# A two-layer decoder trunk on one core: weight loads queued 3 steps further ahead, turned blocks read 5 steps on, a rebuilt layer change, and matmul operands at one place modulo 512 bytes

## The chip, the cores and the metric

The kernel runs on one core of one Trainium2 chip. The metric is the device time of one execution in microseconds, as the median over several runs. A profile of one execution (the page, and the trace behind it) shows what each engine did in it: TensorE (PE, with its weight loads as PEld), VectorE (DVE), ScalarE (ACT), and SyncE (SP), whose queue issues nearly all DMAs here.

## What is computed

256 tokens of width 2048 pass through two layers. Every layer has one input projection (2048 to 4096 columns: branch input, branch gate, memory query, memory gate), a memory attention of 4 heads into 256 memory tokens, a branch mixer (layer 0: trailing-window pooling; layer 1: causal attention of 12 heads, which at 256 tokens is one block), an output projection and a post-norm. Cut to what matters:

```python
h = x
for i in range(2):
    if i == 1:
        k, v = split(h @ w_kv_shared)                  # shared keys and values
    u = h @ w_in[i]
    branch_in, gate_b, mem_q, gate_m = split(u)
    branch = multiscale_pool(branch_in, pool_w, pool_scale) if i == 0 \
        else causal_attention(branch_in, k, v)
    mem_o = memory_attention(mem_q, mem, w_mem_kv[i])  # 4 heads, softmax over 256
    mixed = concat(branch * silu(gate_b), mem_o * silu(gate_m))
    y = mixed @ w_out[i]
    h = layer_norm(1.414 * h + y, ln_g[i], ln_b[i])
```

All of it is float32. Each product is made of three matmuls on operands that are split in two halves: high by high, high by low, low by high.

## The kernel before

**Items.** The weights are read in blocks of 128 partitions by 1024 floats (512 KB). One block is one item, a step of the program's main loop (`run`, L124). An item passes four stations: its load on SP's queue into one of 4 `raw` buffers; a split on ACT (`wh`, L63) and DVE (`wl`, L64) into one of 4 buffer pairs; 12 matmuls of 512 columns on PE (L59); and, after the eighth item of a projection, a consumer of the two finished accumulators. Three tables of numbers set the order: in step `i` the program writes down the split of item `i + LP` (3 ahead), then the load of item `i + LD` (4 ahead), then the matmuls of item `i`, then whatever earlier steps have put off to this one with `later`. Each engine, and SP's queue, runs its part in that order. A split of item `i + 3` needs a free `wh`/`wl` pair, that is, the end of the matmuls of item `i - 1`.

**Turned blocks.** A projection leaves rows of tokens; the next product needs columns. `turned` (L200) transposes 32 by 32 blocks on DVE into a tile `tr` (L184), and `spread` (L186) sends `tr` through DRAM: 4 DMAs out to `via` (L193) one step later, one DMA back (L196) two steps later, into the tile `dd`. Three steps after the transposes the block is read (`put`): split for queries and keys (`to_heads`), or put through tanh for gates (`to_gate`). Softmax weights make the same trip from and into the tile `p`.

**Attention.** `plan` (L380) puts off the stages of a pair of heads from the end of the query projection: scores `a`, exponentials, division, transposes `b`, split `halves` and the product with the values `c`. For memory pairs these are steps 4, 5, 6, 7, 10, 13 and 10, 11, 12, 13, 16, 18.

**Layer change.** After the last output projection of layer 0, `between` (L641) goes through four chunks of 512 columns: it loads gain and bias of the chunk (`ln_load`, on SP's queue), normalises it for both token halves on DVE (`norm_chunk`, two passes each, L422 and L423), transposes it, sends it through DRAM and splits it into `xT`. PE meanwhile works on the 16 items of the memory keys and values of layer 1, which do not need `xT`.

**Output projections.** `out_0` and `out_1` go through one group of 512 columns after the other, 8 items each.

**Place of the tiles.** The tiles lie one behind the other in each partition, each rounded up to 32 bytes. `gap` (384 bytes) puts the activations `xT`, `memT`, `zT` (16384 bytes for each half) at a multiple of 512 bytes. Behind them stand `res`, `ident` and `mask` (multiples of 512 together), `psc` (64), `eps_t` (32), `stats` (256) and `inv` (256): 608 bytes, so `raw`, `wh` and `wl`, and `tr`, `vv`, `kk`, `qq` behind them, begin 96 bytes past a multiple of 512. `ph` and `pl`, behind four more small tiles, begin 224 bytes past one. In the last stretch (`last`, L725) the weights of the final 512 output columns lie in the place of `xT` and `memT`, at a multiple of 512 bytes, and the stationary operand is `zT`, as in the rest of the output projection.

Of the kernel before, what the change touches and what calls it, by code (L numbers as in the profile page):

```python
# [17 lines left out]
P = 128  # L18
# [17 lines left out]
LD = 4  # L36
# [6 lines left out]
def trunk(ctx: ExitStack, tc: tile.TileContext, a: dict, out: bass.AP):  # L43
# [7 lines left out]
    sb.tile([P, 96], F32, name="gap")  # L51
# [134 lines left out]
    def spread(tr, n, first, land):  # L186

        st = {}

        def out():  # L190
            st["via"] = dr.tile([4, 32, 4, n], F32, name="via", bufs=3)
            for i in range(4):
                nc.sync.dma_start(st["via"][:, :, i].rearrange("j r x -> r j x"), tr[32 * i:32 * i + 32, :, :n])  # L193
# [6 lines left out]
    def turned(put, first=1):  # L200
# [20 lines left out]
    def to_heads(dst, first=1):  # L221
        def put(d):
            q = dst()
            split(in_order(q[:, 0]), in_order(q[:, 1]), d)
        return turned(put, first)
# [20 lines left out]
    class Rows:  # L246


        def maxima(self, parts):
            self.nb = sb.tile([P, 4], F32, name="nb", bufs=2)  # L250
            self.sm = sb.tile([P, 4], F32, name="sm", bufs=2)
# [23 lines left out]
    class MemPair(Rows):  # L275
# [19 lines left out]
        def b(self):  # L295
# [7 lines left out]
            spread(tr, 256, 1, lambda: self.d)  # L303
# [20 lines left out]
    class MobaPair(Rows):  # L324
# [24 lines left out]
        def b(self):  # L349
# [6 lines left out]
            spread(tr, 192, 1, lambda: self.d)  # L356
# [44 lines left out]
    def norm_stats(t, n):  # L401
        mv = sb.tile([P, 2], F32, name="mv", bufs=2)
        nc.vector.bn_aggr(mv, stats[:, t, :n].rearrange("p a b -> p (a b)"))
        rs = sb.tile([P, 1], F32, name="rs", bufs=2)
# [23 lines left out]
    psc = sb.tile([P, 12], F32, name="psc")  # L428
    eps_t = sb.tile([P, 4], F32, name="eps_t")
# [7 lines left out]
    def constants():  # L437
        nc.scalar.dma_start(ident, a["ident"])
# [30 lines left out]
    def mem_k(layer, first=1):  # L469
        k = fresh("k", lambda: heads_tile("kk"))  # L470
        proj(memT, halves(a["w_mk"][layer], 0), to_heads(k, first))
# [24 lines left out]
    def mem_q_gate(layer):  # L496
# [5 lines left out]
        def go():  # L502
            plan(prs[0], 4, 7, 10, 13)
            plan(prs[1], 10, 13, 16, 18)
# [94 lines left out]
    def out_0(n):  # L599
        proj(zT, [a["w_out"][0, n, kb] for kb in range(8)], to_residual(n), KORDER)  # L600
# [9 lines left out]
    weave(collect(out_0, 0), mixes[2] + mixes[3], 5)  # L610
    for n in range(1, 4):
        out_0(n)


    gbs = {}

    def ln_load(n):
        gbs[n] = load_gb(n)

    def ln0(n, t):  # L620
        norm_chunk(n, t, gbs[n])

    def h_turn(n):
# [5 lines left out]
        d = {}  # L629

        def land():
            d["d"] = sb.tile([P, 4, 256], F32, name="dd")
            return d["d"]

        def put():
            hi, lo = (in_order(x[:, 4 * n:4 * n + 4]) for x in xT)
            split(hi, lo, d["d"].rearrange("p i (e c) -> p e i c", c=32))
        spread(tr, 256, 1, land)
        later(3, put)

    def between():  # L641
        for n in range(4):
# [6 lines left out]
    mem_k(1, 7)  # L649
# [4 lines left out]
    for grp in range(3):  # L654
# [8 lines left out]
        def go(prs=prs):  # L663
            plan(prs[0], 4, 7, 10, 17)
            plan(prs[1], 10, 14, 18, 20)
# [3 lines left out]


    def out_1():
        for n in range(3):
            proj(zT, [a["w_out"][1, n, kb] for kb in range(8)], to_residual(n), KORDER)

# [4 lines left out]
    def load_gb_rows():  # L679
# [3 lines left out]
        gbt["sel"] = sb.tile([5, 2], F32, name="sel")  # L683
# [13 lines left out]
    for j, it in enumerate(collect(out_1)):  # L697
        items.append(it)
        if j == 0:
# [51 lines left out]
    m0 = sb.tile([P, 2], F32, name="m0")  # L751

# [23 lines left out]
    mv = sb.tile([P, 2], F32, name="mv", bufs=2)  # L776
    nc.vector.bn_aggr(mv, stats[:, 1].rearrange("p a b -> p (a b)"))
    rs = sb.tile([P, 1], F32, name="rs", bufs=2)
# [78 lines left out]
```

## Time and profile before

| | |
|---|---|
| median of 3 runs | 875.21 us (874.09 to 877.88) |
| the profiled execution's own time | 874.49 us |
| its span, first to last instruction | 872.7 us |
| mean granted TensorE clock | 0.979 |
| PE busy | 827.5 us (95% of the span) |
| DVE busy, ACT busy | 550.9 us (63%), 383.4 us (44%) |
| moved by DMA | 193.68 MB, mean 222 GB/s |

The busy time of PE overlaps from matmul to matmul, so how fast it goes is read from the starts of the matmuls, and how long it waits from the view of waits. The view of waits names for each wait the operation that ended it. The chain is the row of operations that ended last, followed back from the end. The granted clock (PEclk) is the share of full speed at which TensorE was allowed to run in a stretch. In the order of a program, rows are instructions of one engine in the order in which they stand, and `x4` is four equal ones; times are never read from it.

### The profile page before, as it was taken

How to read it: one execution, taken by the hardware profiler on the slowest of the kernel's cores; microseconds unless marked ns; L12 is line 12 of the kernel's file. 1: busy time of each engine (PE TensorE's matmuls, PEld its weight loads, DVE VectorE, ACT ScalarE, POOL GpSimd, SP SyncE). 2: the span in 40 equal slices, each digit the busy share in tenths (PEclk: the TensorE clock that was granted, in tenths of full speed). 3: DMA queues.
4: the chain of work that ended last, by engine and by line, in shares of the span. 5: the costliest groups of instructions: out<-in, count | busy, mean ns of one | idle time of the engine just before them, and what ended most of it. 6: DMA issues, size and time to landing. Idle time of an engine off the chain costs nothing.

```text
span 872.7 us, 10083 instructions
## 1 busy us (share of the span) xinstructions
PE 827.5 (95%) x3670; PEld 668.5 (77%) x3670; DVE 550.9 (63%) x705; ACT 383.4 (44%) x476; POOL 0.2 (0%) x4
## 2 busy tenths in 40 slices
PE   7999998999999999987899899999999998999996
PEld 6868786887788788865678678888788887888885
DVE  6655665668765655766565565675467654678746
ACT  6543443444544433423544454444345443445520
POOL 0000000000000000000000000000000000000000
PEclk9999999999999999999999989999999998999998
DMA  8877568766788665587875686777767676776842
GB/s 311 274 223 226 181 200 274 231 204 207 225 269 286 223 190 187 157 260 223 274 239 172 199 258 223 224 230 227 222 192 232 207 234 209 223 238 194 294 138 97
DMA packets 96117, 193.68 MB, mean 222 GB/s; under 512 B 8639, under 2 KB 31423, under 8 KB 95807
## 3 DMA queue, kind: packets, MB, share of 16 engines
q1 hardware_dynamic: 94800, 190.61, 69.0%
q10 hardware_dynamic: 1268, 2.44, 0.9%
q8 instruction: 28, 0.46, 0.2%
q14 instruction: 21, 0.17, 0.1%
HBM read 173.36 MB, written 19.66 MB: 221 GB/s over the span
## 4 chain that ended last, share of the span: by engine, by line
PE 61%; DMA 19%; DVE 10%; ACT 4%; SPq 3%; issue 3%; DVEq 0%; ACTq 0%
PE acc L59 58%; DMA via<-tr 6%; DMA raw<-in_w_in 5%; DVE wl L64 4%; DMA dd<-via 3%; SPq L193 3%; ACT wh L63 3%; DVE tr L184 2%; PE o L59 2%; PE s L59 2%; DMA raw<-in_w_mv 1%; DMA p<-via 1%; DMA raw<-in_w_mk 1%; DMA raw<-in_w_out 1%; DMA raw<-in_w_sk 1%
## 5 line engine op out<-in xcount | busy, mean ns | idle before, releaser
L64 DVE TENSOR_TENSOR wl<-raw,wh 128x1024 fp32r<-128x1024 f32 (+2 forms) x272 | 323.8, 1197 | 239.5 <-ACT wh L63 237.1
L63 ACT ACTIVATE wh<-raw 128x1024 fp32r<-128x1024 f32 (+2 forms) x272 | 280.9, 1038 | 340.7 <-PE acc L59 144.3
L59 PE MATMUL acc<-wl,xh 128*128 128x512 f32 x704 | 281.6, 400 | 5.1 <-DVE wl L64 5.1
L59 PE MATMUL acc<-wh,xh 128*128 128x512 f32 x704 | 281.8, 400 | 3.4 <-ACT wh L63 3.4
L59 PE MATMUL acc<-wh,xl 128*128 128x512 f32 x704 | 281.2, 400 | 0.0
L59 PEld LDWEIGHTS acc<-wl,xh 128*128 128x128 f32 x704 | 134.3, 191 | 39.8 <-DVE wl L64 8.0
L59 PEld LDWEIGHTS acc<-wh,xh 128*128 128x128 f32 x704 | 134.4, 191 | 36.2 <-ACT wh L63 4.7
L59 PEld LDWEIGHTS acc<-wh,xl 128*128 128x128 f32 x704 | 134.1, 190 | 32.3
L59 PE MATMUL acc<-wh,zl 128*128 128x512 f32 x224 | 88.7, 396 | 0.5 <-DVE zl L64 0.5
L59 PE MATMUL acc<-wl,zh 128*128 128x512 f32 x224 | 88.8, 396 | 0.0
L59 PE MATMUL acc<-wh,zh 128*128 128x512 f32 x224 | 88.2, 394 | 0.0
L59 PE MATMUL acc<-wh,mh 128*128 128x512 f32 (+1 forms) x130 | 53.3, 410 | 8.2 <-ACT wh L63 8.2
L59 PE MATMUL acc<-wl,mh 128*128 128x512 f32 (+1 forms) x130 | 53.2, 409 | 4.8 <-DVE wl L64 4.8
L59 PE MATMUL acc<-wh,ml 128*128 128x512 f32 (+1 forms) x130 | 52.4, 403 | 0.0
L59 PEld LDWEIGHTS acc<-wh,zl 128*128 128x128 f32 x224 | 42.1, 188 | 10.8 <-DVE zl L64 0.9
L59 PEld LDWEIGHTS acc<-wl,zh 128*128 128x128 f32 x224 | 42.1, 188 | 10.2
L59 PEld LDWEIGHTS acc<-wh,zh 128*128 128x128 f32 x224 | 42.1, 188 | 10.2
L59 PEld LDWEIGHTS acc<-wh,mh 128*128 128x128 f32 x130 | 25.8, 198 | 15.6 <-ACT wh L63 9.9
L59 PEld LDWEIGHTS acc<-wl,mh 128*128 128x128 f32 x130 | 25.6, 197 | 12.2 <-DVE wl L64 6.6
L59 PEld LDWEIGHTS acc<-wh,ml 128*128 128x128 f32 x130 | 25.7, 198 | 5.8
L184 DVE STREAM_TRANSPOSE tr<-acc 128x512 f32<-128x512 f32 x42 | 27.6, 693 | 1.3 <-PE acc L59 1.3
L63 ACT ACTIVATE zh<-zf 128x256 fp32r<-128x256 f32 x32 | 13.0, 415 | 31.4 <-DVE zf L272 26.7
(130 smaller groups left out, 532.7 us busy)
## 6 DMA issues: line engine op xcount, KB each, us to landing
raw<-in_w_in SPq DMA_DIRECT2D x128, 512.0 KB, 5.9
raw<-in_w_out SPq DMA_DIRECT2D x64, 512.0 KB, 4.4
via<-tr SPq DMA_DIRECT2D x116, 128.0 KB, 2.6
dd<-via SPq DMA_DIRECT2D x25, 512.0 KB, 4.4
raw<-in_w_sk SPq DMA_DIRECT2D x24, 512.0 KB, 5.6
raw<-in_w_sv SPq DMA_DIRECT2D x24, 512.0 KB, 5.1
raw<-in_w_mk SPq DMA_DIRECT2D x14, 512.0 KB, 5.6
raw<-in_w_mv SPq DMA_DIRECT2D x13, 512.0 KB, 5.8
```

The costliest lines, as they stand in the source:

```text
L59: nc.tensor.matmul(o, l, r, start=start, stop=stop)
L63: nc.scalar.activation(hi, src, AF.Copy)
L64: nc.vector.tensor_sub(lo, src, f(hi))
L184: nc.vector.transpose(dst, src)
L193: nc.sync.dma_start(st["via"][:, :, i].rearrange("j r x -> r j x"), tr[32 * i:32 * i + 32, :, :n])
```

## The change

1. `LD` goes from 4 to 7: in step `i` the load of item `i + 7` is written down, with the 4 `raw` buffers as they were.
2. `spread` writes the 4 DMAs out at once, in the step of the transposes, and the DMA back one step later. `turned` reads the block 5 steps after the transposes.
3. `plan` takes two numbers: scores at `a`, transposes at `a + 3`, `halves` at `a + 8`, the product with the values at `c`. Memory pairs: 6 and 16, 15 and 25; layer 1's pairs: 6 and 17, 15 and 25.
4. The layer change no longer normalises with gain and bias ahead of the turn. ACT normalises the chunk in place (`normed`, two instructions of 128 by 512 per chunk); it is transposed and sent through DRAM into the `gate` or `p` tile; ACT applies gain and bias there by column (`affine`, four instructions of 128 by 256 per chunk, from the new tile `gcol`), and the split follows a step later. The rows of `res` get gain and bias on DVE (`ln_rows`, four instructions per chunk) from step 20 on, and the loads for that stand at step 18 on. `gcol` is filled near the program's start by two DMAs on ACT's queue that read single floats.
5. The first two column groups of an output projection are interleaved (`out_cols`): 6 items of the one, 6 of the other, then the last two of each, which read the parts of `zT` that are finished last. The load of the final norm's rows moves from the first item to the eleventh.
6. `gap`, and the small tiles `nb`, `sm`, `mv`, `rs`, `m0` and `sel`, go; `psc` (64 bytes), `eps_t` (32), `gcol` (128) and one tile `small` (160) that holds the others stand ahead of `xT`: 384 bytes, as much as `gap` had. What is left between `mask` and `raw` is `stats` and `inv`, 512 bytes, so `raw`, `wh`, `wl`, `tr`, `vv`, `kk`, `qq`, `p`, `gate`, `ph` and `pl` all begin at a multiple of 512.

```diff
-LD = 4
+LD = 7
...
-    sb.tile([P, 96], F32, name="gap")
+    psc = sb.tile([P, 12], F32, name="psc")
+    eps_t = sb.tile([P, 4], F32, name="eps_t")
+    gcol = sb.tile([P, 2, KT], F32, name="gcol")
+    small = sb.tile([P, 40], F32, name="small")
...
-    def spread(tr, n, first, land):
+    def spread(tr, n, land):
...
-        later(first, out)
-        later(first + 1, back)
+        out()
+        later(1, back)
...
-                spread(st["tr"], 256, first, land)
-                later(first + 2, lambda: put(st["d"].rearrange("p i (e c) -> p e i c", c=32)))
+                spread(st["tr"], 256, land)
+                later(5, lambda: put(st["d"].rearrange("p i (e c) -> p e i c", c=32)))
...
-    def plan(pr, a, b, h, c):
+    def plan(pr, a, c):
...
-        later(b, pr.b)
-        later(h, pr.halves)
+        later(a + 3, pr.b)
+        later(a + 8, pr.halves)
         later(c, pr.c)
...
-            plan(prs[0], 4, 7, 10, 13)
-            plan(prs[1], 10, 13, 16, 18)
+            plan(prs[0], 6, 16)
+            plan(prs[1], 15, 25)
...
+        for i, nm in enumerate(("ln_g", "ln_b")):
+            nc.scalar.dma_start(gcol[:, i], a[nm][0].rearrange("(k p) -> p k", p=P))
...
+    def out_cols(layer, *ns, extra=()):
+        cols = [collect(proj, zT, [a["w_out"][layer, n, kb] for kb in range(8)], to_residual(n), KORDER)
+                for n in ns]
+        for c in cols:
+            items.extend(c[:6])
+        items.extend(extra)
+        for c in cols:
+            items.extend(c[6:])
...
-    weave(collect(out_0, 0), mixes[2] + mixes[3], 5)
-    for n in range(1, 4):
-        out_0(n)
+    main = collect(out_cols, 0, 0, 1)
+    items.extend(main[:5] + mixes[2] + mixes[3] + main[6:11] + main[5:6] + main[11:])
+    for n in range(2, 4):
+        out_cols(0, n)
...
+    def normed(n):
+        for t in range(2):
+            r = res[:, t, n * 512:(n + 1) * 512]
+            nc.scalar.activation(r, r, AF.Identity, scale=mvs[:, t, 2:3], bias=mvs[:, t, 3:4])
...
+        def affine():
+            for m in range(4):
+                y = d[:, :, m * 64:(m + 1) * 64]
+                nc.scalar.activation(y, y, AF.Identity, scale=gcol[:, 0, 4 * n + m:4 * n + m + 1],
+                                     bias=gcol[:, 1, 4 * n + m:4 * n + m + 1])
...
-        spread(tr, 256, 1, land)
-        later(3, put)
+        spread(tr, 256, lambda: d)
+        later(5, affine)
+        later(6, put)
...
-            later(3 * n, lambda n=n: ln_load(n))
-            later(1 + 3 * n, lambda n=n: ln0(n, 0))
-            later(2 + 3 * n, lambda n=n: ln0(n, 1))
+            later(1 + 3 * n, lambda n=n: normed(n))
             later(2 + 3 * n, lambda n=n: h_turn(n))
+            later(18 + 4 * n, lambda n=n: gbs.setdefault(n, load_gb(n)))
+            later(20 + 4 * n, lambda n=n: ln_rows(n, gbs[n]))
```

The order of SP's queue at the layer change, where the memory keys of layer 1 (`w_mk`) give way to the memory values (`w_mv`). Before, `ln_g` and `ln_b` are the gain and bias of a chunk, `via<-tr` the 4 DMAs out of a turned chunk, `dd<-via` its DMA back:

```order
L92 DMA raw<-in_w_mk 128x2x512 x4
L414 DMA ln_g<-in_ln_g 128x512
L414 DMA ln_b<-in_ln_b 128x512
L92 DMA raw<-in_w_mk 128x2x512 x3
L414 DMA ln_g<-in_ln_g 128x512
L414 DMA ln_b<-in_ln_b 128x512
L193 DMA via<-tr 32x4x256 x4
L92 DMA raw<-in_w_mk 128x2x512
L196 DMA dd<-via 128x1024
L94 DMA raw<-in_w_mv 128x1024 x2
```

The same place now; the chunk's DMA back lands in `gate` or `p`:

```order
L99 DMA raw<-in_w_mk 128x2x512 x8
L101 DMA raw<-in_w_mv 128x1024
L200 DMA via<-tr 32x4x256 x4
L101 DMA raw<-in_w_mv 128x1024
L203 DMA gate<-via 128x1024
L101 DMA raw<-in_w_mv 128x1024 x2
L200 DMA via<-tr 32x4x256 x4
L101 DMA raw<-in_w_mv 128x1024
L203 DMA p<-via 128x1024
```

The first chunk's DMAs out stood behind 7 loads of `w_mk` and two pairs of gain and bias; they now stand behind all 8 and the first of `w_mv`, and the gain and bias have left the place.

ACT's order at the same place. Before, `rs` is the root of the variance, `wh<-raw` the split of an item, `xh<-dd` that of a turned chunk:

```order
L405 ACT_TABLE_LOAD
L405 ACTIVATE rs<-mv,eps_t 128x1 x2
L63 ACTIVATE wh<-raw 128x1024 x5
L63 ACTIVATE xh<-dd 128x1024
L63 ACTIVATE wh<-raw 128x1024 x3
L63 ACTIVATE xh<-dd 128x1024
```

Now; `res<-res,small` is `normed`, `gate<-gate,gcol` and `p<-p,gcol` are `affine`:

```order
L410 ACTIVATE small<-small,eps_t 128x1 x2
L70 ACTIVATE wh<-raw 128x1024
L637 ACTIVATE res<-res,small 128x512 x2
L70 ACTIVATE wh<-raw 128x1024 x3
L637 ACTIVATE res<-res,small 128x512 x2
L70 ACTIVATE wh<-raw 128x1024 x3
L637 ACTIVATE res<-res,small 128x512 x2
L651 ACTIVATE gate<-gate,gcol 128x4x64 x4
L70 ACTIVATE wh<-raw 128x1024
L70 ACTIVATE xh<-gate 128x1024
L70 ACTIVATE wh<-raw 128x1024 x2
```

The first turned chunk is split behind 8 item splits instead of 5, and 6 instructions of `normed` and 4 of `affine` stand ahead of it.

More of the change, by code (lines that the diff above doesn't have):

```diff
@@ L196, in back, with turned @@
             nc.sync.dma_start(land(), st["via"].rearrange("j r i x -> (j r) i x"))
-        later(first, out)
-        later(first + 1, back)
-    def turned(put, first=1):
+        out()
+        later(1, back)
+    def turned(put):
         st = {}
@@ L219, in in_order, with to_heads @@
         return tile.rearrange("p a (t i c) -> p (a t) i c", t=2, i=4)
-    def to_heads(dst, first=1):
+    def to_heads(dst):
         def put(d):
@@ L224, in put @@
             split(in_order(q[:, 0]), in_order(q[:, 1]), d)
-        return turned(put, first)
+        return turned(put)
     def to_gate(dst):
@@ L302, in b @@
             self.d = self.p.rearrange("p j n -> p (j n)").rearrange("p (i x) -> p i x", i=4)
-            spread(tr, 256, 1, lambda: self.d)
+            spread(tr, 256, lambda: self.d)
         def halves(self):
@@ L467, in val_tile, with mem_k @@
         return sb.tile([P, 2, 2, 512], F32R, name="vv")
-    def mem_k(layer, first=1):
+    def mem_k(layer):
         k = fresh("k", lambda: heads_tile("kk"))
-        proj(memT, halves(a["w_mk"][layer], 0), to_heads(k, first))
+        proj(memT, halves(a["w_mk"][layer], 0), to_heads(k))
     def mem_v(layer):
@@ L609, in trunk, with ln_rows @@
     after(load_x)
-    weave(collect(out_0, 0), mixes[2] + mixes[3], 5)
-    for n in range(1, 4):
-        out_0(n)
[L615 to L621, printed above, removed]
+    main = collect(out_cols, 0, 0, 1)
+    items.extend(main[:5] + mixes[2] + mixes[3] + main[6:11] + main[5:6] + main[11:])
+    for n in range(2, 4):
+        out_cols(0, n)
+    def ln_rows(n, gb):
+        for t in range(2):
+            r = res[:, t, n * 512:(n + 1) * 512]
+            later(t, lambda r=r: nc.vector.tensor_tensor(r, r, gb[0], op=ALU.mult))
+            later(t, lambda r=r: nc.vector.tensor_add(r, r, gb[1]))
+    def normed(n):
+        for t in range(2):
+            r = res[:, t, n * 512:(n + 1) * 512]
+            nc.scalar.activation(r, r, AF.Identity, scale=mvs[:, t, 2:3], bias=mvs[:, t, 3:4])
     def h_turn(n):
@@ L628, in h_turn @@
                    res[:, t, n * 512:(n + 1) * 512].rearrange("p (m j c) -> p m j c", m=4, j=4))
[L629 to L633, printed above, removed]
+        d = sb.tile([P, 2, 512], F32, name="p") if n % 2 else gate_tile()
+        d = d.rearrange("p a b -> p (a b)").rearrange("p (i x) -> p i x", i=4)
+        def affine():
[3 more added lines that the diff above has]
+                                     bias=gcol[:, 1, 4 * n + m:4 * n + m + 1])
         def put():
             hi, lo = (in_order(x[:, 4 * n:4 * n + 4]) for x in xT)
-            split(hi, lo, d["d"].rearrange("p i (e c) -> p e i c", c=32))
-        spread(tr, 256, 1, land)
-        later(3, put)
+            split(hi, lo, d.rearrange("p i (e c) -> p e i c", c=32))
+        spread(tr, 256, lambda: d)
+        later(5, affine)
+        later(6, put)
     def between():
+        for t in range(2):
+            nc.vector.scalar_tensor_tensor(mvs[:, t, 3:4], mvs[:, t, 0:1], -1.0, mvs[:, t, 2:3],
+                                           op0=ALU.mult, op1=ALU.mult)
+        gbs = {}
         for n in range(4):
-            later(3 * n, lambda n=n: ln_load(n))
-            later(1 + 3 * n, lambda n=n: ln0(n, 0))
-            later(2 + 3 * n, lambda n=n: ln0(n, 1))
+            later(1 + 3 * n, lambda n=n: normed(n))
             later(2 + 3 * n, lambda n=n: h_turn(n))
+            later(18 + 4 * n, lambda n=n: gbs.setdefault(n, load_gb(n)))
+            later(20 + 4 * n, lambda n=n: ln_rows(n, gbs[n]))
     after(between)
-    mem_k(1, 7)
+    mem_k(1)
     mem_v(1)
@@ L695, in split_rows @@
                                        op0=ALU.mult, op1=ALU.add)
-    for j, it in enumerate(collect(out_1)):
+    main = collect(out_cols, 1, 0, 1) + collect(out_cols, 1, 2)
+    for j, it in enumerate(main):
         items.append(it)
-        if j == 0:
+        if j == 10:
             after(load_gb_rows)
```

29 lines of the change are left out of this document (11 added, 18 removed).

## The prediction

> **What bounds the kernel now.** I read the busy shares first, then who PE waited for, then the clock that PE was granted, then the starts of single matmuls.
>
> ```profile
> span 872.7 us, 10083 instructions
> PE 827.5 (95%) x3670; PEld 668.5 (77%) x3670; DVE 550.9 (63%) x705; ACT 383.4 (44%) x476; POOL 0.2 (0%) x4
> ```
>
> PE is the bound: it is busy for 95% of the span, and the 45.2 us without a matmul are the first thing to explain. The view of waits for PE alone (what was waited for: total us, times, longest):
>
> ```profile
> PE acc L59 <- ACT wh L63: 11.6, 7, 5.0
> PE acc L59 <- DVE wl L64: 10.0, 11, 1.5
> PE o L59 <- ACT ph L63: 6.5, 2, 4.0
> PE s L59 <- ACT qq L63: 3.0, 3, 1.5
> PE s L59 <- DVE qq L64: 2.9, 4, 0.8
> PE pt L788 <- DVE cc L785: 2.7, 1, 2.7
> PE o L59 <- DVE pl L64: 2.2, 2, 1.5
> PE acc L59 <- DVE zl L64: 0.5, 1, 0.5
> ```
>
> So 21.6 us are waits for split weights (`wh`, `wl`), 8.7 for split softmax weights (`ph`, `pl`), 5.9 for queries and keys (`qq`), 0.5 for a late `zl`: 36.7 us in the body. The 2.7 us (`pt`) belong to the tail, which the change leaves as it is.
>
> The second loss is the clock. Seven stretches have half the granted clock; here are the first, the last and the sum (us, PE busy and matmuls, PEclk, DMA share, GB/s):
>
> ```profile
> 92.70:96.10 3.40, 3.40 (x11) 0.50 0.55 173
> ...
> 731.00:737.80 6.80, 6.50 (x20) 0.50 0.41 149
> sum 30.60, PE 28.04; mean PE 4.01
> ```
>
> PE worked 28.0 us at half speed, so at full speed the same work takes 14.0 us less. Each stretch stands behind waits; the smallest waits that had one behind them are those of 86 to 96 us:
>
> ```profile
> PE s L59 <- ACT qq L63: 0.8, 1, 0.8
> PE s L59 <- DVE qq L64: 0.8, 1, 0.8
> ```
>
> 1.6 us of waits were enough. The Trainium skill ("TensorE: Matmul & The Clock Gate", Part 1) says that the clock falls to half behind an idle window of about 3.4 us; by that rule the short waits would cost no clock, a version with only short waits left would get back all 14.0, and the sum below would be 1.7 us lower. The rows above show half clock behind less. I keep one such stretch below.
>
> The third is the pace of the matmuls at full clock. Rows of the timeline, start and duration, with the many between left out: a stretch of the output projection, and one of the last 512 columns.
>
> ```profile
> 790.05 0.39 PE L59 MATMUL acc<-wh,zh 128*128 128x512 f32 x1
> ...
> 828.55 0.39 PE L59 MATMUL acc<-wh,zh 128*128 128x512 f32 x1
> ```
>
> ```profile
> 842.53 0.39 PE L59 MATMUL acc<-xh,zh 128*128 128x512 f32 x1
> ...
> 850.69 0.39 PE L59 MATMUL acc<-xl,zh 128*128 128x512 f32 x1
> ```
>
> 38.50 us hold 165 matmuls, 0.700 us for each three (high-high, high-low, low-high). 8.16 us hold 36, 0.680 for each three. Both have the same width, the same stationary tiles `zh` and `zl` and one weight load per matmul; what differs is where the moving operand lies: `wh` and `wl` 96 bytes past a multiple of 512, `xT` and `memT` on one. It isn't the traffic, as two stretches without any DMA show:
>
> ```profile
> 99.50:104.40 4.90, 4.90 (x22) 1.00 0.00 0
> 843.00:847.76 4.76, 4.76 (x23) 1.00 0.00 0
> ```
>
> 4.90 us are seven threes at 0.700 and 4.76 seven at 0.680 (the counts hold one or two cut at the edges).
>
> **The change part by part.** *Place.* The matmuls that get the new place are counted in the costliest groups (one of the three kinds each):
>
> ```profile
> L59 PE MATMUL acc<-wl,xh 128*128 128x512 f32 x704 | 281.6, 400 | 5.1 <-DVE wl L64 5.1
> ...
> L59 PE MATMUL acc<-wl,zh 128*128 128x512 f32 x224 | 88.8, 396 | 0.0
> ...
> L59 PE MATMUL acc<-wl,mh 128*128 128x512 f32 (+1 forms) x130 | 53.2, 409 | 4.8 <-DVE wl L64 4.8
> ```
>
> 704 + 224 + 130 = 1058 threes, by 0.020 us: 21.2 us. Those at half clock gain less (about 20 threes, 0.4 us), so -21. All of it lies on the path, since PE is the bound, as long as the weights keep up: an item then takes 4 x 0.680 = 2.72 us instead of 2.80. Attention and pooling matmuls (256 and 128 columns) change place too; I take 0 for them, since no row pairs them.
> The Trainium skill speaks against this term: "SBUF — State Buffer" (Operand start alignment) gives the multiple of the element size as the rule for a start and calls it a matter of legality, with no speed measured, and "TensorE: Matmul & The Clock Gate" (Part 2, step 1) says that loading weights doesn't take read bandwidth from the running matmul. By these the term is 0; the 0.700 and 0.680 decide for 21.
>
> *Loads further ahead.* The largest waits are at the layer change. SP's queue there, from the timeline, and the chain behind it:
>
> ```profile
> 368.52 1.76 SPq L193 DMA_DIRECT2D via<-tr  x4
> ```
>
> ```profile
> 370.39 5.11 DMA raw<-in_w_mk
> ...
> 375.61 1.07 ACT wh L63
> ...
> 376.70 1.22 DVE wl L64
> ```
>
> The 4 DMAs out must wait for the transposes, take 1.76 us to issue, and only then comes the load; 5.11 us later ACT can split it, and PE waits for that. With `LD` 7 the loads up to item `j + 7` stand ahead of the DMAs out of step `j`. What holds a load then is its `raw` buffer: that of `j + 7` is free when item `j + 3` is split, about 1.07 + 1.22 = 2.3 us after the matmuls of `j - 1` end. The transposes of step `j` end an item and about 0.7 us after those matmuls (3.4), 1.1 us after the load could go, so the load is not what the DMAs out wait for. ACT can take the data of `j + 7` only four items after those matmuls (10.9 us), 8.6 us after the buffer came free; that covers the 5.11. Of the 21.6 us I take all away but 2.
>
> *Turned blocks later.* A round trip of a query block, from the chain:
>
> ```profile
> 717.51 0.68 DVE tr L184
> ...
> 722.68 6.22 DMA dd<-via
> ...
> 730.02 1.24 DVE qq L64
> ...
> 731.29 2.51 PE s L59 x10
> ```
>
> From the end of the transposes (718.2) to the scores 13.1 us pass. The scores stood 4 steps on (4 x 2.80 = 11.2 us) and now stand 6 steps on (6 x 2.72 = 16.3); less 0.7 for the transposes that leaves 2.5 us to spare, and the 5.9 us go. Softmax weights likewise: `halves` is 5 steps behind the transposes where it was 3 in memory pairs, and the values 2 or more behind that, so the 8.7 go. The `zl` wait (0.5) goes with the interleaved columns, which put five items between the last pooling product and its reader. ACT and DVE no longer stand still for these blocks; what is late next is the round trip itself, if it grows by over 2.5 us.
>
> *Layer change.* DVE loses 16 normalising passes there and gets 16 later; ACT gets 8 `normed` and 16 `affine`. The nearest rows:
>
> ```profile
> L422 DVE SCALAR_TENSOR_TENSOR res<-res,mv,ln_g 128x512 f32<-128x512 f32 x8 | 5.9, 741 | 0.0
> L63 ACT ACTIVATE vv<-acc 128x512 fp32r<-128x512 f32 x10 | 5.7, 593 | 6.5 <-PE acc L59 6.5
> L554 ACT ACTIVATE res<-dd 128x256 f32<-128x256 f32 x12 | 4.0, 406 | 2.6 <-DMA dd<-via 2.6
> L63 ACT ACTIVATE wh<-raw 128x1024 fp32r<-128x1024 f32 (+2 forms) x272 | 280.9, 1038 | 340.7 <-PE acc L59 144.3
> L64 DVE TENSOR_TENSOR wl<-raw,wh 128x1024 fp32r<-128x1024 f32 (+2 forms) x272 | 323.8, 1197 | 239.5 <-ACT wh L63 237.1
> ```
>
> ACT: 8 x 0.593 + 16 x 0.406 = 11.2 us more. Over the 17 items of the change (46.2 us) it has 17 x 1.04 for weights, 5 x 1.06 for turned blocks, 1.2 for values and 11.2: 35.4, or 77%. It has room, and what covers a late split is the two items (5.4 us) that are split ahead. DVE gets at most 16 x 0.74 = 11.9 us between steps 20 and 33, beside 14 x 1.20 = 16.8 for weights and, at its mean for all else ((550.9 - 323.8) / 872.7 = 26% of 38.1 us), 9.9: 38.6 of 38.1 us. That is the new tight spot; its cover is again 5.4 us, and I charge 1 us for it (bounds: 0, and 5 if it falls behind by as much again as the cover).
>
> *Rest.* `gcol` adds 4096 reads of 4 bytes near 16 us. The nearest row is the load of `psc`:
>
> ```profile
> psc<-in_pool_scale ACTq DMA_DIRECT2D x1, 6.0 KB, 4.8
> ```
>
> 4.8 us to land, beside weight loads that left PE no wait there: between 0 and 2 us, I take 0, since nothing reads it for 300 us.
>
> *Sum.* Against the profiled execution: 872.7 - 21 (place) - 33.7 (36.7 of waits less 3 kept) - 12.3 (14.0 of clock less one stretch of 3.4 us, 1.7) = 805.7 us of span. That execution took 874.49, 1.8 more than its span, and the median is 0.7 above it: 808.2, so 808.
>
> **The rivals.** *The place does nothing*: `wh` and `wl` keep 0.700 wherever they lie, and the 0.680 has another cause, such as the last weights' lying in one piece: 808 + 21 = 829. Against it stand the same stationary tiles and the two stretches without DMA; for it, that only one stretch shows the pace. 12%. (The two pages named above would give this time.)
>
> *The layer change still waits*, now for ACT or DVE. Its waits were these (356 to 425 us):
>
> ```profile
> PE acc L59 <- DVE wl L64: 6.3, 7, 1.5
> PE acc L59 <- ACT wh L63: 4.8, 4, 1.6
> ```
>
> If they stay, with the two half-clock stretches there (3.3 us), it is 808 + 11.1 + 3.3 - 2 = 820. 12%.
>
> *The loads don't get earlier*, because 4 `raw` buffers hold them anyway and the change doesn't do what it says: the 21.6 us stay, with three stretches (5 us): 808 + 26.6 - 2 - 1.7 = 831. Against it, the load at 370.39 stood right behind the DMAs out. 7%.
>
> *Slower: the round trips jam.* If ACT and DVE fall so far behind that a split comes only just ahead of its matmuls, the load of `j + 7` comes after the transposes of `j`, and every DMA out waits for a load. 35 round trips stand in the program (25 into `dd`, 10 into `p`). The change gains 67 us, so it decides from 67 / 35 = 1.9 us of PE per trip on; one item each (2.72) gives 35 x 2.72 = 95, and 808 + 95 = 903. For it speaks only that `raw` stays at 4; against it, DVE at 63% and ACT at 44%. 4%.
>
> **How the numbers follow.** The forecast has 65%, with 803 (all waits and all clock gone: 3 + 1.7 us less) to 815 (twice the kept waits, the tight spot at its upper bound) as its own bounds. The range reaches over the layer change and the place: 801 to 831, the lower end 2 us further since one execution can be as much off the median. It leaves out the jam and about half of the loads' rival. 0.5% is about what a measurement of this kernel can tell from no change. Every case but the jam ends faster: faster 0.95, the same 0.01, slower 0.04.
>
> **What would show it.** Right: threes of matmuls 0.680 us apart on `wh` and `wl`; PE's waits for `wh` and `wl` under 4 us, for `qq`, `ph`, `pl` near 0; one or no half-clock stretch between 11 and 800 us; loads on SP's queue that wait for a split and not behind `via`. Wrong: threes still 0.700 apart (place); waits for `wh` and `wl` of 10 us or more near 360 to 410 us (layer change) or spread over the program (loads); DMAs out that stand behind a waiting load, and scores that wait for `qq` (jam).

## The result and the profile after

The changed kernel takes **832.18 us** (median, 831.5 to 833.63), the kernel before 875.12 in the same measurement: a ratio of 0.9507, 95% interval 0.9481 to 0.9533. It is faster by 43 us, but 24 above the 808 forecast and 1 above the upper end of the range. The profiled execution took 833.63 us, and its span is 830.4, at a mean granted clock of 0.987 (before 0.979).

First the page of the kernel after:

```profile
span 830.4 us, 10089 instructions
...
PE 797.4 (96%) x3670; PEld 663.6 (80%) x3670; DVE 547.5 (66%) x707; ACT 394.8 (48%) x500; POOL 0.2 (0%) x4
```

PE is still the bound, for 96% of a shorter span. A share of busy time can't tell whether the remaining 4% could go, so the next view is again PE's waits, now from 20 us on, so that the start is apart (what was waited for: total us, times, longest):

```profile
PE acc L66 <- DVE wl L71: 9.7, 8, 3.8
PE s L66 <- DVE qq L71: 6.4, 1, 6.4
...
PE acc L66 <- ACT wh L70: 2.3, 4, 1.3
PE pt L66 <- DVE zf L584: 1.8, 1, 1.8
PE s L66 <- ACT qq L70: 0.4, 1, 0.4
```

20.6 us are left in the body. The waits for `ph`, `pl` and `zl` went as forecast; those for `qq` (6.8 us) and for split weights (12.0) did not. They are few and long now: one of 6.4 and one of 3.8 make half of the 20.6. One is new, the 1.8 us for `zf`, where VectorE reads a product of the pooling.

The waits in the first 20 us, before and after:

```profile
PE acc L59 <- ACT wh L63: 5.0, 1, 5.0
```

```profile
PE acc L66 <- ACT wh L70: 4.4, 1, 4.4
```

This is the one wait for the first weights of the program. Nothing can be loaded ahead of it. The forecast had it among the waits that go.

The half clock, in the stretches of the kernel after (us, PE busy, PEld, DVE, ACT, POOL, PEclk, DMA share, GB/s):

```profile
263.30:266.70 3.40, 3.40 (x18) 3.40 (x17) 2.97 (x6) 2.42 (x3) 0.00 (x0) 0.50 0.84 294
430.50:440.70 10.20, 6.02 (x19) 5.25 (x20) 7.92 (x9) 3.02 (x5) 0.00 (x0) 0.50 0.56 192
781.70:785.20 3.50, 3.50 (x11) 2.75 (x10) 2.52 (x3) 1.96 (x2) 0.00 (x0) 0.56 0.84 262
sum 17.10, PE 12.92 PEld 11.40 DVE 13.41 ACT 7.40 POOL 0.00; mean PE 4.31 PEld 3.80 DVE 4.47 ACT 2.47 POOL 0.00
```

PE worked 12.9 us in these stretches, nearly all of it at half speed, so 6.5 us are lost; before it was 14.0.

The pace, in the output projection of the kernel after (start, duration):

```profile
788.52 0.39 PE L66 MATMUL acc<-wh,zh 128*128 128x512 f32 x1
...
798.04 0.39 PE L66 MATMUL acc<-wh,zh 128*128 128x512 f32 x1
```

9.52 us hold 14 threes: 0.680 each, where the kernel before needed 0.700 at this place.

Against the forecast's sum, in its own terms, then:

| term | forecast | in the profile | how read |
|---|---|---|---|
| place | -21 | -20.1 | mean from start to start of 512-column matmuls without a wait: 0.2332 to 0.2269 us |
| waits | -33.7 | -11.7 | 36.7 less the 20.6 and 4.4 above |
| half clock | -12.3 | -7.5 | 14.0 less 6.5 |
| span | -67 | -42.3 | 872.7 less 830.4 |

The three terms leave 3.0 us that none of them holds. The place is as forecast. Of the missing 24.7 us of span, 22.0 are waits, 4.8 half clock and 0.9 place, and the 3.0 that no term holds go the other way.

**The two longest waits.** VectorE ahead of the wait of 6.4 us (start, duration, and in brackets how long the engine was idle before and what ended that):

```profile
422.54 1.22 DVE L71 TENSOR_TENSOR wl<-raw,wh 128x1024 fp32r<-128x1024 f32 x1
429.55 0.69 DVE L631 TENSOR_TENSOR res<-res,ln_g 128x512 f32<-128x512 f32 x1 [5.79 <-DMA ln_g<-in_ln_g]
431.66 0.69 DVE L632 TENSOR_TENSOR res<-res,ln_b 128x512 f32<-128x512 f32 x1 [1.42 <-DMA ln_b<-in_ln_b]
...
433.41 1.22 DVE L71 TENSOR_TENSOR qq<-dd,qq 128x1024 fp32r<-128x1024 f32 x1
```

VectorE works in order. It came to `ln_rows`, the gain and bias that the rebuilt layer change now puts on the residual rows later, and stood 5.8 + 1.4 us for their DMAs. In the program these are written down two steps ahead of their use. SyncE's queue shows when they were issued:

```profile
419.06 0.39 SPq L99 DMA_DIRECT2D raw<-in_w_in  x1
422.81 0.34 SPq L203 DMA_DIRECT2D dd<-via  x1
423.24 0.39 SPq L99 DMA_DIRECT2D raw<-in_w_sk  x1
423.68 0.46 SPq L419 DMA_DIRECT2D ln_g<-in_ln_g  x1
424.19 0.42 SPq L419 DMA_DIRECT2D ln_b<-in_ln_b  x1
```

SyncE works in order too. It stood 3.2 us until a DMA out had landed, so that the DMA back (`dd<-via`) could go, and came to `ln_g` at 423.68, just as VectorE finished the split ahead of `ln_rows` (422.54 + 1.22). `ln_g` then took 5.8 us to land and `ln_b` 7.4, where their medians in the kernel before are 3.7 and 3.8. The two steps of the program had become no time at all. The split of the queries stood behind that, and PE behind the split: 6.4 us, and then the stretch of 10.2 us at half clock.

The wait of 3.8 us lies at 777 us. The windows of 764 to 781 us (same columns as above):

```profile
764.00:781.00 17.00, 12.25 (x54) 9.48 (x53) 16.72 (x23) 9.28 (x11) 0.00 (x0) 1.00 0.56 189
```

VectorE is busy for 16.72 of 17 us and PE only for 12.25. Two columns of the residual, which now end close together because they are interleaved, the ordinary splits, and `split_rows` (the splits of the final norm's rows), whose start the change moved from the 1st to the 11th item, fall on the same 17 us.

**The beginning.** ScalarE's queue in the kernel after, with an issue of a DMA as `ACTq`:

```profile
15.86 0.44 ACTq L442 DMA_DIRECT2D gcol<-in_ln_g  x1
16.34 4.34 ACTq L442 DMA_DIRECT2D gcol<-in_ln_b  x1
20.71 1.29 ACTq L443 DMA_DIRECT2D ident<-in_ident  x1
...
23.62 1.06 ACT L70 ACTIVATE wh<-raw 128x1024 fp32r<-128x1024 f32 x1 [6.72 <-issue]
```

Of the two DMAs that fill `gcol` with single floats, the first is issued in 0.44 us; the second holds ScalarE for 4.34 us, and `ident` behind it for 1.29 (0.39 before). No weights are split for 6.7 us, and raw buffers come free late. From start to start of the matmuls PE loses 5.3 us between 23 and 71 us through it.

### The profile page after: what moved, and what is told of

It is laid out like the page before. It is cut to its first block, busy times and chain, and to the rows that moved or that the text cites. A ratio compares the mean times of both kernels' runs of the same rounds, so it can differ in the third digit from the quotient of the medians.

```text
span 830.4 us, 10089 instructions
## 1 busy us (share of the span) xinstructions
PE 797.4 (96%) x3670; PEld 663.6 (80%) x3670; DVE 547.5 (66%) x707; ACT 394.8 (48%) x500; POOL 0.2 (0%) x4
## 3 DMA queue, kind: packets, MB, share of 16 engines
q10 hardware_dynamic: 5396, 2.46, 1.2%
## 4 chain that ended last, share of the span: by engine, by line
PE 76%; DMA 13%; DVE 6%; issue 2%; ACT 2%; ACTq 1%; SPq 1%; DVEq 0%
PE acc L66 71%; DMA raw<-in_w_in 4%; DVE wl L71 3%; DMA via<-tr 2%; PE s L66 2%; PE o L66 2%; DMA raw<-in_w_mv 2%; DMA ln_b<-in_ln_b 2%; ACT wh L70 1%; DMA res<-in_w_mv 1%; DMA raw<-in_w_out 1%; DMA raw<-in_xT 1%; ACTq L442 1%; DVE xl L71 0%; PE pt L66 0%
## 5 line engine op out<-in xcount | busy, mean ns | idle before, releaser
L66 PE MATMUL acc<-wl,xh 128*128 128x512 f32 x704 | 275.5, 391 | 3.9 <-DVE wl L71 3.9
L66 PE MATMUL acc<-wh,xh 128*128 128x512 f32 x704 | 275.5, 391 | 1.8 <-ACT wh L70 1.8
L66 PE MATMUL acc<-wh,xl 128*128 128x512 f32 x704 | 274.6, 390 | 0.0
L66 PEld LDWEIGHTS acc<-wl,xh 128*128 128x128 f32 x704 | 132.6, 188 | 32.6 <-DVE wl L71 5.9
L66 PEld LDWEIGHTS acc<-wh,zh 128*128 128x128 f32 x224 | 42.3, 189 | 8.8
L66 PEld LDWEIGHTS acc<-wh,mh 128*128 128x128 f32 x130 | 25.3, 195 | 10.2 <-ACT wh L70 5.3
L66 PEld LDWEIGHTS acc<-wl,mh 128*128 128x128 f32 x130 | 25.3, 194 | 7.2 <-DVE wl L71 2.1
L66 PEld LDWEIGHTS acc<-wh,ml 128*128 128x128 f32 x130 | 25.3, 194 | 5.0
```

Of the source, the lines that this page charges most:

```text
L66: nc.tensor.matmul(o, l, r, start=start, stop=stop)
```

## The experiments

Two questions were tried in turn: what parts of the change do alone, and where the missing 24 us went. The later reads and the interleaved columns were not run alone. To compare kernels, the time from 11 us to the tail (its first matmul) is split into three: the matmuls at their pace (each at the mean from start to start that its width has at full clock without a wait), what is lost at full clock beyond that, and what is lost in half-clock stretches, waits there included. These sums over all matmuls are worked out from the starts in each kernel's one trace, whose execution need not be the median one (that of the place alone is the slowest of four, 865.74 us):

| kernel | ratio to before (95%) | pace | lost at full clock | lost in half-clock stretches |
|---|---|---|---|---|
| before | 1 | 798.5 | 31.2 | 21.9 |
| place alone | 0.988 (0.983 to 0.994) | 778.9 | 44.6 | 19.1 |
| changed | 0.951 (0.948 to 0.953) | 778.4 | 18.8 | 12.5 |
| changed, loads 6 ahead | 0.960 (0.953 to 0.966) | 777.8 | 25.3 | 13.0 |
| changed, loads 8 ahead | 0.979 (0.970 to 0.988) | 777.6 | 32.7 | 25.1 |
| changed, five places mended | 0.926 (0.923 to 0.930) | 777.8 | 9.2 | 0.0 |

**The place alone** (`place_only`): the kernel before with the weights' tiles at a multiple of 512 bytes.

```diff
-    sb.tile([P, 96], F32, name="gap")
+    psc = sb.tile([P, 12], F32, name="psc")
+    eps_t = sb.tile([P, 4], F32, name="eps_t")
+    sb.tile([P, 72], F32, name="gap")
```

> The kernel before, with only the place of the tiles changed: the weights' halves begin at a multiple of 512 bytes. Place theory: 1058 threes of matmuls 0.020 us shorter, threes 0.680 us apart on the weights' tiles, 875 - 21 = 854 us (851 to 857), the waits and half-clock stretches about as before. Rival (the pace of the last 512 columns had another cause, the changed kernel's pace comes from its order): threes stay at 0.700 and the time at 875.

860.5 us (859.35 to 865.74). Every three takes 0.680, and the pace gives 19.6 us, about as in the whole change (20.1). But 13.4 us more are lost at full clock and 2.8 less in half-clock stretches, so the time falls by 1.2% only, some 10 us, and misses the 851 to 857 expected. PE's largest waits from 20 us on:

```profile
PE acc L61 <- DVE wl L66: 14.9, 16, 3.0
PE o L61 <- ACT ph L65: 8.2, 3, 3.9
PE acc L61 <- ACT wh L65: 6.2, 6, 2.1
```

They were 10.0, 6.5 and 6.6 before; all PE's waits in the body grew from 31.7 to 38.8 us, about half of the 13.4. A faster PE asks for each block 0.08 us sooner per item, so what came just in time would come late; that is an argument, no run separates it. The gain of the place exists, but about half of it was lost again here.

**The loads alone** (`ld7_only`): the kernel before with one number changed.

```diff
-LD = 4
+LD = 7
```

> The kernel before, with only the loads 7 steps ahead instead of 4. Theory A (late loads made the waits for split weights): PE's waits for wh and wl fall from 21.6 to under 10 us, and with the clock behind them the time falls by 10 to 18 us, to 857 to 865; the blocks, still read 3 steps on, may wait longer. Rival B (4 raw buffers hold the loads anyway): 875, nothing changes. Rival C (more loads in flight make every DMA out and back land later): waits for qq and ph grow by more than the others fall, over 875.

942.81 us (940.46 to 947.65), a ratio of 1.0805 (1.0739 to 1.0871): 70 us slower. SyncE's largest waits in the kernel before, and in this one:

```profile
SPq L193 <- DVE tr L184: 150.0, 29, 10.6
SPq L94 <- DVE wl L64: 139.7, 69, 5.0
SPq L92 <- DVE wl L64: 122.4, 63, 3.8
```

```profile
SPq L92 <- DVE wl L64: 261.9, 103, 7.9
SPq L94 <- DVE wl L64: 202.9, 86, 7.8
```

Before, SyncE waited for transposes ahead of DMAs out. Now it stands before loads whose `raw` buffer isn't free yet: 464.8 us for `wl` against 262.1. Such waits alone need not hurt, for the changed kernel has 370.6 us of them; what matters is what stands behind them. Here DMAs out queue behind such loads, since the old kernel writes them down one step later, behind the load of `j + 8`. Who pays is seen on ScalarE:

```profile
ACT ph L63 <- DMA p<-via: 63.1, 10, 10.9
ACT xh L63 <- DMA dd<-via: 43.9, 4, 11.4
ACT qq L63 <- DMA dd<-via: 36.0, 5, 8.2
ACT kk L63 <- DMA dd<-via: 34.2, 5, 8.6
```

The blocks come back late, ScalarE stands in order before each of them (63.1 us for `ph`, 9.9 before; 221.1 for all blocks that come back, 44.0 before), and the splits of the weights queue behind it. This is the forecast's jam. Of the answers expected C is the nearest (over 875), but the waits for split weights didn't fall at all: 36.4 us from 20 us on, 16.6 before.

**The rest without the loads** (`after_ld4`): the changed kernel with `LD` at 4 again.

```diff
-LD = 7
+LD = 4
```

> The changed kernel with the loads 4 steps ahead, as before. Theory A: the loads stand behind the DMAs out again, waits for wh and wl grow by 8 to 20 us, 842 to 855 us. Rival C (the loads far ahead are what makes the transports slow, 4.3 us for a DMA out against 2.6 before): DMAs out land in about 3 us again and the time is 832 or less.

935.27 us (933.06 to 947.01), 1.0755 times the kernel before (1.0665 to 1.0845): far more than theory A's 842 to 855. Of C's answer only the landing of a DMA out came true, not the time. ScalarE's wait for weights, and on the page the landing of a DMA out (KB each, median us):

```profile
ACT wh L70 <- DMA raw<-in_w_in: 175.1, 79, 8.4
```

```profile
via<-tr SPq DMA_DIRECT2D x116, 128.0 KB, 2.3
```

The same wait in the kernel before:

```profile
ACT wh L63 <- DMA raw<-in_w_in: 103.0, 75, 6.6
```

With DMAs out written down in the step of their transposes, 4 loads stand ahead of them; the load of `j + 5` has to wait for the transposes. So the loads starve, though a DMA out itself lands in 2.3 us, faster than the 4.3 of the changed kernel: landing times don't set the time here. The loads alone cost 70 us, all the rest without them 62, and together they gain 43. That in the rest it is the DMAs out written one step sooner that cost is read from these waits; they were not run alone.

**One load less, one more** (`after_ld6`, `after_ld8`): the changed kernel with `LD = 6` and `LD = 8`.

> The changed kernel with loads 6 steps ahead in place of 7. Reading Q (what counts is how many loads stand ahead of a DMA out: 4 starve the splits, 8 wait for raw buffers ahead of the DMA out): with 6 loads ahead the time lies a little above that of 7 or at it, 830 to 850, and transfers land no later than with 7. Rival (more loads in flight is always better for the splits, and each step taken away costs a third of the 103 us between 7 and 4): 860 to 870.

> The changed kernel with loads 8 steps ahead. Reading Q: the load of j + 8 stands ahead of the DMAs out of step j and waits for the raw buffer of j + 4, which is split only when step j is over, so the DMAs out start an item or more late; as in the kernel before with loads 7 ahead, the round trips jam: over 880, with SyncE's waits for wl over 350 us and ScalarE's put waits (dd, p) over 80 us. The read 5 steps on covers part of that: if it covers all, 832 to 840. Rival (four raw buffers hold the loads whatever the queue says): 830 to 834.

839.06 us (836.2 to 840.35) and 855.5 (852.86 to 858.13). With 6, as the first reading had it; losing a third of the 103 us with each step is refuted. With 8 the jam is there, but at 23 us over the changed kernel, between both answers: SyncE's waits with 8,

```profile
SPq L99 <- DVE wl L71: 226.8, 92, 8.4
SPq L101 <- DVE wl L71: 182.5, 89, 7.5
```

add up to 409.3 us for `wl` (370.6 with 7). What ScalarE waits for all blocks that come back is the clearer sign: nothing with 4 and with 6, 24.6 us with 7, 102.4 with 8, and 221.1 in the kernel before with `LD` 7, where 8 loads stand ahead of a DMA out too. That less than half of the jam is left here may be due to the later reading; no run separates it from the rest. The runs fit one reading: what counts is how many loads stand ahead of a DMA out. 4 starve the splits, 8 hold up the round trips, 6 and 7 lie between; whether 6 or 7 is better they don't decide, since the two intervals touch.

**The old layer change** (`layer_old`): all else as changed. Of `h_turn` and `between`:

```diff
-        later(5, affine)
-        later(6, put)
+        later(5, put)
...
-            later(1 + 3 * n, lambda n=n: normed(n))
+            later(3 * n, lambda n=n: gbs.setdefault(n, load_gb(n)))
+            later(1 + 3 * n, lambda n=n: norm_chunk(n, 0, gbs[n]))
+            later(2 + 3 * n, lambda n=n: norm_chunk(n, 1, gbs[n]))
...
-            later(18 + 4 * n, lambda n=n: gbs.setdefault(n, load_gb(n)))
-            later(20 + 4 * n, lambda n=n: ln_rows(n, gbs[n]))
```

> The changed kernel with the old layer change: gains and offsets loaded by SyncE one item before VectorE uses them, VectorE does both passes of each half column, the turned blocks are split without ScalarE's pass, and nothing comes later for the residual. Place, loads 7 ahead, reads 5 steps on and interleaved columns stay as changed. Theory S (a transfer that an engine waits for in order takes 7 us or more to land now, since it stands in line with seven loads, and one item is 2.72 us): VectorE stands 4 to 5 us at each of the four columns, the splits behind it are late by more than the two items' cover, and the layer change costs 8 to 20 us more; the waits at 428 to 441 us (11 us with the clock) don't come. Sum 829 to 841. The book of the prediction (12.4 us of waits and clock at the layer change come back, everything else as it is): 844 less the 11, 833. Rival: the order of the layer change was never what waited, only the loads were: 821, as with the spread loads of gains.

837.77 us (834.43 to 838.59), a ratio of 0.9577 (0.9521 to 0.9633). The interval touches that of the changed kernel, so a gain of the rebuilt layer change is likely by the medians (0.7%) and not certain. The time lies in theory S's range and, at the edge, can't be told from the 833 of the prediction's own sum; the rival's 821 is refuted. The trace is plainer. VectorE, 356 to 445 us, and PE in the same window:

```profile
DVE res L427 <- DMA ln_g<-in_ln_g: 15.9, 3, 5.9
...
DVE res L428 <- DMA ln_b<-in_ln_b: 3.4, 3, 1.5
```

```profile
PE acc L66 <- DVE wl L71: 14.5, 4, 6.6
```

The same in-order wait for the same kind of load, only earlier. The kernel before has no wait of VectorE for `ln_g` or `ln_b`; with its `LD` at 7 it has 13.1 us, so the loads queued further ahead bring them. Against this run, the rebuilt layer change took the wait away at 356 to 400 us and made it anew from 400 us on, 15.2 us of VectorE in all with the longest at 428. PE's waits in the window are 10.5 us in the changed kernel and 11.1 in the kernel before.

**Five places mended.** If the missing time is five local waits, each should go by a local edit; if transfers as a whole are short, a wait taken away would come back elsewhere.

Gains loaded and used further apart (`fix_rows`):

```diff
-            later(18 + 4 * n, lambda n=n: gbs.setdefault(n, load_gb(n)))
-            later(20 + 4 * n, lambda n=n: ln_rows(n, gbs[n]))
+            later(18 + 8 * n, lambda n=n: gbs.setdefault(n, load_gb(n)))
+            later(24 + 8 * n, lambda n=n: ln_rows(n, gbs[n]))
```

> The changed kernel with the loads of the final norms' gains and offsets (512 columns each) spread to every eighth item instead of every fourth, and each made use of six items after its load instead of two. Theory S (the 24 us by which the forecast was too low come from five separate places at which an engine that works in order stands at a transfer or a long piece of work that was put too close): the waits of 6.5 us and the half clock of 10.2 us behind them at 428 to 441 us of the span go, and the wait at 406 us; the time falls by 9 to 13 us, to 819 to 823 (ratio to the kernel before about 0.94). Theory D (transfers as a whole are the limit now, with seven steps of loads in flight, and a wait that is taken away at one place turns up at another): the fall is under 3 us, about 830, and the waits of TensorE for the splits stay at 16 us in all, at other places.

824.38 us (819.16 to 825.79), a ratio of 0.9434 (0.9388 to 0.948). PE's wait for `qq` at 428 us is gone, and so is the stretch of half clock behind it. The interval is just clear of the changed kernel's; the gain, 6 us by the ratios and 8 by the medians, is under the 9 to 13 expected, since smaller waits come at 458 to 489 us.

The first norm's gains in one piece (`fix_gcol`; the host lays them out as the tile wants them):

```diff
-        for i, nm in enumerate(("ln_g", "ln_b")):
-            nc.scalar.dma_start(gcol[:, i], a[nm][0].rearrange("(k p) -> p k", p=P))
+        nc.scalar.dma_start(gcol, a["gcol"])
```

> The changed kernel with the gains and offsets of the first norm laid out in memory as the tile wants them, and loaded by one DMA of one piece for each partition instead of two DMAs of single floats. Theory S: ScalarE's queue is no longer held at this issue for 4.3 us at 16 us of the span, the identity's copy and the first turns come earlier, SP's loads go on, and the small waits at 24.7, 48.3, 56.8 and 69.4 us (5.4 us in all) go: 826 to 828. Theory D: the loads come late at the beginning whatever the gains do, and the fall is under 2 us.

824.92 us (822.5 to 826.72), 0.9458 (0.9421 to 0.9495). The final rows of the second block (`fix_gb`) begun twelve items later:

```diff
-            later(5 + n, lambda n=n: split_rows(f(raw)[:, n * 512:(n + 1) * 512], n))
+            later(17 + n, lambda n=n: split_rows(f(raw)[:, n * 512:(n + 1) * 512], n))
```

> The changed kernel with the splits of the second block's gains and offsets into rows begun twelve items later, so that VectorE doesn't have them between two columns of the residual. Theory S: the waits of 5.2 us at 770 to 781 us of the span go, and with them part of the 3.4 us of half clock behind them: 824 to 827. Theory D: VectorE is as full twelve items later and the waits are found there: 830 to 833.

822.62 us (821.57 to 828.54), 0.9438 (0.9391 to 0.9486). The same window as above, 764 to 781 us, in this kernel:

```profile
764.00:781.00 17.00, 17.00 (x76) 13.97 (x75) 13.75 (x15) 9.57 (x9) 0.00 (x0) 1.00 0.80 262
```

PE is busy throughout. By the ratios these two gain 4 and 6 us, about as theory S expected. But their intervals still touch that of the changed kernel: their traces show that the wait in question went, their times alone don't prove it.

All five (`fix_all`): the three edits, and two more that were only run here:

```diff
-    after(load_x)
+    after(lambda: later(6, load_x))
...
-            later(1 + 3 * n, lambda n=n: normed(n))
-            later(2 + 3 * n, lambda n=n: h_turn(n))
+            later(1 + 4 * n, lambda n=n: normed(n))
+            later(2 + 4 * n, lambda n=n: h_turn(n))
```

> The changed kernel with five edits together: the two loads and splits of gains above, the gains of the first norm in one piece, the loads of the block's input six items later, and the normed columns and their turns after the layer change every fourth item instead of every third. Theory S: the sum of the five places, 24 us less what is left of the half clock: 804 to 812 (ratio 0.92 to 0.93). Theory D: over 824.

**808.24 us** (806.85 to 810.93), a ratio of 0.9263 (0.923 to 0.9297), clear of the changed kernel's. PE's waits from 20 us on, the tail left out:

```profile
PE acc L66 <- DVE wl L71: 4.7, 7, 1.5
...
PE o L66 <- DVE pl L71: 0.2, 1, 0.2
```

From start to start, us lost at each place:

| where in the changed kernel | lost | with its own edit | with all five |
|---|---|---|---|
| 23 to 71 us, `gcol` | 5.3 | 0.2 | 0.3 |
| 260, loads of the block's input beside a DMA out | 1.9 | | 0 |
| 384 to 408, eight DMAs out in one step | 4.7 | | 2.1 |
| 427 to 435, `ln_rows` | 7.2 | 0 | 0 |
| 770 to 781, VectorE full | 5.3 | 0 | 1.0 |

So the missing time was local, and the waits don't move elsewhere, apart from 4.5 us at 445 to 487 us, which come with the spread loads of gains (the kernel with that edit alone loses 4.1 there, the others under 1). That transfers as a whole are the limit (theory D, over 824) is refuted by the 808.24; with all five, the whole 787 us before the tail run at full clock. For the second and third place the cause was only argued from the trace, since their edits didn't run alone. The third is also not one place: 1.8 of its 4.7 us lie at 406, where VectorE stood for the first `ln_g` and `ln_b`, and these went with `fix_rows`, so that `ln_rows` cost 9.0 us, half clock aside.

**Where the tiles lie.** `off256` and `off64`: the changed kernel with 256 and 64 bytes put between `inv` and `raw`, so that `raw`, `wh`, `wl` and the tiles behind them are that far past a multiple of 512. The activations stay on one.

```diff
     nc.vector.memset(eps_t[:, 0:1], EPS)
+    sb.tile([P, 64], F32, name="pad")    # off64: 16
     scr = res.rearrange("p a b -> p (a b)")
```

> The changed kernel with raw, wh, wl and all tiles behind them 256 bytes past a multiple of 512, the stationary activations still on one. If 512 is the period, threes of matmuls are over 0.680 us apart (0.69 to 0.72); if a smaller period (256, 128 or 64 bytes) is all that counts, they stay at 0.680 and the time within 2 us of the changed kernel's 832.

> The changed kernel with every tile behind the small ones 64 bytes past a multiple of 512. If what slows a matmul's moving operand is any offset from 256 bytes: threes 0.700, time 850. If it is an offset from 64 bytes (96 past is on 32): threes 0.680, time 832.

827.08 and 832.71 us, one run each. The pace is read from the starts, with 256 and with 64:

```profile
780.95 0.39 PE L66 MATMUL acc<-wh,zh 128*128 128x512 f32 x1
...
784.35 0.39 PE L66 MATMUL acc<-wh,zh 128*128 128x512 f32 x1
```

```profile
784.91 0.39 PE L66 MATMUL acc<-wh,zh 128*128 128x512 f32 x1
...
788.34 0.39 PE L66 MATMUL acc<-wh,zh 128*128 128x512 f32 x1
```

Five threes take 3.40 and 3.43 us: 0.680 each at 256, 0.686 at 64. The operand need not lie on 512, 256 is as good, and 64 bytes cost a third of what the 96 of the kernel before cost. Neither of the two paces expected for 64 was right. Times of one run each can't show such a difference: 0.006 over 1058 threes is 6 us.

## Why the prediction was wrong

*Place: right.* 20.1 us for a forecast 21, by 0.020 per three. The rival that the place does nothing is refuted by the kernel with the place alone. The Trainium skill's "SBUF — State Buffer" (Operand start alignment) speaks of legality and timed nothing, so it isn't contradicted; what failed is the term of 0 that the prediction drew from it as the other answer. One condition in that step carried more than it seemed to: "as long as the weights keep up". Alone, 10.6 of the 19.6 us were lost again elsewhere.

*Loads: half right.* The loads did get earlier (SyncE waits for splits, not behind `via`). "Of the 21.6 us I take all away but 2" failed for three reasons. First, 5.0 of the 21.6 were the start of the program; the total of a line in the view of waits was read as if all of it lay in the body, though a window of the first 20 us would have shown it. That is 4.4 us of the miss. Second, 4.8 us of splits late at 770 to 781 have nothing to do with loads. Third, the beginning and the spots at 384 to 408 us left 7.2, 1.6 of it behind VectorE's wait for the first `ln_g` and `ln_b`.

*Turned blocks: right for `ph`, `pl` and `zl`, and for `qq` undone by another step.* All 8.7 + 0.5 us went. Of the 5.9 us for `qq` nothing went on balance, since 6.8 came anew, 6.4 of it at one place, and not from a round trip that grew by 2.5 us, but from VectorE.

*Layer change: the step that failed most.* "That is the new tight spot; its cover is again 5.4 us, and I charge 1 us for it (bounds: 0, and 5 ...)" weighed how much work VectorE has between steps 20 and 33, and found 38.6 in 38.1 us. What it left out is that `ln_rows` waits in order for a DMA. That DMA is written down two items (5.4 us) earlier, but in SyncE's queue it stood behind a DMA back and loads, was issued when VectorE was already there, and took 5.8 and 7.4 us to land. VectorE stood 7.2 us, more than the cover, PE 6.4, and half clock came on top: 10.2 us lost by the starts at this place, for the 1 us charged. The question to ask was not how long the instruction takes, but what it waits for.

*What had no price, or the wrong one.* `gcol` was put at 0, "since nothing reads it for 300 us", with 2 as the bound. Nobody did wait for the data; ScalarE waited for the issue, and 5.3 us went. The nearest row, the load of `psc`, was a time to landing and couldn't show that. The move of the final norm's rows from the 1st to the 11th item was not costed at all: 5.3 us and a stretch of half clock.

*Clock.* One stretch was kept, three came; each stands behind one of the waits above. With those gone no stretch is left before the tail, so this term followed the waits. The Trainium skill ("TensorE: Matmul & The Clock Gate", Part 1) asks for an idle window of about 3.4 us: here 3.4 us of half clock stand behind a wait of 1.8 us at 260, so a shorter wait was enough, as in the kernel before. The length of one wait doesn't decide it either: 1.6 us at 406 had no half clock behind it.

*The rivals.* The time came out at that of the loads' rival (831), but not by its mechanism. The layer change "still waits, now for ACT or DVE" is the nearest to what happened; it had 12%, and it was priced with the waits of before instead of a new one. That its size came out nearly right there (10.5 us of waits for the 11.1 of before) is luck. The jam, at 4%, is refuted for the whole change and real for its half: its place and mechanism were right (DMAs out behind loads that wait for a buffer), and what keeps it away, as far as the runs show, is that the DMAs out were written down a step sooner, with 7 loads ahead of them and not 8. The prediction counted that but never named it as its protection.

With five places mended the time is the forecast's, 808.24 us, but that is partly luck. Of the terms, 9.3 us of waits are left for the 3 forecast (4.4 of them at the start), no half clock for 1.7, and 3 us again lie in no term; the traced execution of that kernel took 810.93.

## What to carry to other kernels

An in-order engine waits for whatever its next instruction needs, so an instruction that depends on a transfer is priced by when that transfer lands in the new queue, not by its own duration. A queue depth and the places of what shares the queue are one setting: here the loads alone cost 8%, all the rest without them 7.5%, and together they gained. And a total of waits is cut by windows before it is promised away: the start of a program stays.

## What the runs showed of the hardware

- The pace of a 512-column matmul on these operands follows where the moving operand starts: 0.680 us for a three at 0 and at 256 bytes past a multiple of 512, 0.686 at 64, 0.700 at 96 (256 and 64 from one trace each).
- DMAs of single floats can cost their issuer. 4.34 us of ScalarE's queue went for 2048 floats of `ln_b`, issued right behind 2048 of `ln_g`, which took 0.44; why the second and not the first, no run shows. ScalarE's DMA queue had 5396 packets where the kernel before, and so its variant with `LD` 7, had 1268:

```profile
q10 hardware_dynamic: 5396, 2.46, 1.2%
```

The Trainium skill ("DMA: Bandwidth & Descriptors", Rules for kernel authors) says that such a pattern becomes one descriptor for each element and should be laid out contiguously; the 4128 additional packets for 4096 floats agree, and with one piece the issue took 0.39 us.
- The landing of a DMA out goes with how many loads are queued ahead of it in the changed kernel: a median of 2.3 us with 4 and with 6, 4.3 with 7, 4.8 with 8. With 7 it is 3.4 with the old layer change and 3.7 with the five places mended, so the number of loads isn't all.
